# 20 blocks of u of each layer split by ScalarE and GpSimd during the scores, candidate sums by segments, a third PSUM bank for u

## The chip, the cores and the metric

One core of one Trainium2 chip runs the whole program. The metric is device time in microseconds, from one launch to its end. The engines are TensorE (PE; its weight loads PEld), VectorE (DVE), ScalarE (ACT), GpSimd (POOL) and SyncE (SP), which only issues DMA.

## The reference

One inference step of two layers for 512 prompt tokens and 8 sample tokens of width 1024. A layer is a mixer, a layer norm, PEER, and a layer norm. Layer 0 mixes with gated DeltaNet and RG-LRU, layer 1 with sliding-window attention. PEER looks experts up by product keys:

```python
q = (tb @ w_q).reshape(PEER_BLOCK, PEER_HEADS, 2, PEER_D_SUB)
s = jnp.einsum('thcd,hcnd->thcn', q, sub_keys).astype(F32)
s_top, i_top = lax.top_k(s, PEER_TOPK)
cand = (s_top[:, :, 0, :, None] + s_top[:, :, 1, None, :]).reshape(PEER_BLOCK, PEER_HEADS, -1)
cand_idx = (i_top[:, :, 0, :, None] * PEER_N_KEYS + i_top[:, :, 1, None, :]).reshape(
    PEER_BLOCK, PEER_HEADS, -1)
best, pos = lax.top_k(cand, PEER_TOPK)
expert = jnp.take_along_axis(cand_idx, pos, axis=-1)
gate = jax.nn.softmax(best, axis=-1)
act = jax.nn.gelu(jnp.einsum('td,thkd->thk', tb, u_tab[expert]).astype(F32))
return jnp.einsum('thk,thkd->td', (gate * act).astype(tb.dtype), v_tab[expert])
```

There are 8 heads of 2 halves, 128 keys a half, top 16 of each, and 16384 experts (rows of `u_tab` and `v_tab`).

## The kernel before

**Precision.** A float32 matrix is used as a float16 high half and a float16 low half: `split` copies the source, scaled, to the high half on ScalarE (`wh`), and VectorE subtracts to get the low half (`wl`). `mm3` then makes three float16 matmuls (L86 to L88) in place of one.

**PEER for most tokens is dense.** For the first 384 tokens all 128 blocks of u (128 experts each) are multiplied with the tokens: `u_step` takes one block, 24 matmuls of 384 columns into one PSUM bank of the pool `pu` (2 buffers), and ScalarE's gelu writes `act`. The gates of these tokens are spread to a dense table in DRAM (`GD`), in 12 parts of 32 tokens (`gates`): VectorE builds one-hot rows `oh` (L486 to L489), TensorE multiplies them into `pg` (64 matmuls of 128 columns a part), ScalarE copies `pg` eight times to the single buffer `stage`, and a DMA on ScalarE's queue stores `stage` to `GD`. Later the main loop multiplies gate times activation with blocks of v into `yps` (L607), and does the blocks of u that are left, one an iteration. The last 128 prompt tokens and the 8 samples fetch their rows instead: 136 lists of 128 rows for u and as many for v, each by one indirect DMA that GpSimd issues (L357), with a dot product (L364) or a multiply-add on VectorE for each list.

**The order of a layer.** The mixer; the scores (16 steps `hc`: a projection by a block of `wq`, loaded two steps ahead and split, then the product with the keys, `psc`, copied to `scs`, then the top 16 on VectorE, `topk_half`); then `topk_pairs` six times (once for the samples, twice with 4 heads, three times with 8): it makes the 50 candidate sums (`cand`, L256) and index sums (`ce`, L260), one add for each first index and segment, and the lookup of the 16 best. Between them `run_u` does 3, 3, 3 and 7 blocks of u; 7 more stand ahead of each later `pairs`. In `gates` three blocks of u are spread over a part (`UG` is 3). The tile framework orders each engine's instructions when it builds, by its own estimate, so blocks of u move up and down against this text; an engine then runs its list strictly in order.

**The presplit.** `NPRE` is (16, 12): that many blocks of u of a layer are split during the mixer, in quarters, to `ppr`, and stored to DRAM (`PW`) as halves (L106 load of `pst`, L110 store). `ublock` loads these as halves (`wpr`); a later block is loaded as float32 (`wst`) and split when it is needed. All these loads and stores are issued by SyncE, one after the other.

## Time and profile before

| | us |
|---|---|
| median of 3 runs | 3012.0 (3011.1 to 3014.87) |
| the profiled execution | 3010.7 |
| its span, first to last instruction | 3008.9 |
| TensorE busy | 2845.8 (95%) |
| VectorE busy | 2569.4 (85%) |
| ScalarE busy | 1319.3 (44%) |
| GpSimd busy | 856.1 (28%) |
| mean granted clock of TensorE | 0.98 |

Ends of matmuls are modelled, so TensorE's busy time is not time at its peak. The clock is the share of 2.4 GHz that was granted; it has two levels, 1.2 and 2.4 GHz, so a mean of 0.93 is 14% of a stretch at the lower one. In a row of the table by stretch stand the stretch and its length, then busy time and count of instructions for each engine. In a row of one line or tile stand the shortest, median and longest duration in ns and the first and last start in us. In a row of waits stand the waiting instruction, what ended the wait, the total in us, how often, and the longest. A chain that ended last is followed back from the last instruction, at each step to what released it.

### The profile page before, as it was taken

The numbers are of one execution on the slowest core, as the hardware profiler recorded it, in microseconds if no ns is written. First come the engines' busy times: TensorE is split into PE (matmuls) and PEld (weight loads), VectorE is DVE, ScalarE is ACT, GpSimd is POOL, SyncE is SP. The second block draws the span as 40 slices with busy tenths as digits, with TensorE's granted clock in tenths as the row PEclk, the third lists the DMA queues.
The fourth block names the chain that finished last, engine by engine and source line by source line (L and its number), as shares of the span: only waits on it lengthen the run. The fifth ranks groups of instructions, "written<-read, shape, count | busy, mean of one in ns | idle before, by whom it ended". The sixth has DMA issues, their size and how long they took to land.

```text
span 3008.9 us, 49598 instructions
## 1 busy us (share of the span) xinstructions
PE 2845.8 (95%) x18198; PEld 1726.9 (57%) x18198; DVE 2569.4 (85%) x5871; ACT 1319.3 (44%) x2171; POOL 856.1 (28%) x662
## 2 busy tenths in 40 slices
PE   8979999899999999999998899989999999999998
PEld 7768586456655555544446559645665555554443
DVE  6756789999978988889995879989987898898998
ACT  4743332356753333333335743335765333333342
POOL 2300101310024555435520000130002555454552
PEclk9999999999999999999999999999999999999999
DMA  4264424866699999999977422686569999999996
GB/s 136 72 218 149 147 86 161 295 238 217 217 339 390 366 354 363 363 358 370 352 276 246 154 79 85 211 293 213 193 216 327 390 360 360 353 359 359 362 357 234
DMA packets 332104, 798.78 MB, mean 265 GB/s; under 512 B 28611, under 2 KB 165259, under 8 KB 328020
## 3 DMA queue, kind: packets, MB, share of 16 engines
q1 hardware_dynamic: 241004, 442.78, 43.5%
q0 software_dynamic: 78336, 285.25, 25.5%
q10 hardware_dynamic: 12520, 67.58, 6.1%
q8 instruction: 142, 2.33, 0.3%
q14 instruction: 102, 0.84, 0.1%
HBM read 700.96 MB, written 93.17 MB: 264 GB/s over the span
## 4 chain that ended last, share of the span: by engine, by line
PE 66%; DVE 13%; DMA 10%; ACT 6%; issue 4%; POOL 1%; SPq 0%; ACTq 0%; DVEq 0%; POOLq 0%
PE yps L607 30%; PE pu L88 7%; PE pu L86 7%; PE pu L87 7%; DMA row<-in_u_rows,elist 2%; ACT stage L72 2%; PE pq L87 2%; DMA GD<-stage 2%; PE pq L86 2%; PE pq L88 2%; DVE wl L81 2%; DMA pst<-in_uT 2%; DVE row L364 1%; DMA PW<-ppr 1%; DMA gl<-GD 1%
## 5 line engine op out<-in xcount | busy, mean ns | idle before, releaser
L607 PE MATMUL yps<-vv,vw 128*128 128x512 f16 x4536 | 1010.8, 379 | 10.3 <-ACT vv L72 8.1
L607 PEld LDWEIGHTS <-vw 128*128 128x128 f16 x4608 | 450.4, 98 | 542.2 <-issue 17.0
L357 POOL DMA_INDIRECT row<-in_v_rows,elist x272 | 395.4, 1454 | 862.9 <-issue 251.0
L88 PE MATMUL pu<-xh,wl 128*128 128x384 f16 x1824 | 598.4, 329 | 34.2 <-DVE wl L81 33.7
L86 PE MATMUL pu<-xh,wh 128*128 128x384 f16 x1824 | 598.9, 328 | 15.6 <-ACT act L333 10.7
L87 PE MATMUL pu<-xl,wh 128*128 128x384 f16 x1824 | 598.4, 328 | 0.0
L357 POOL DMA_INDIRECT row<-in_u_rows,elist x272 | 389.1, 1430 | 679.8 <-DVE best L237 250.3
L72 ACT ACTIVATE wh<-wst 128x1024 f16<-128x1024 f32 x296 | 312.4, 1056 | 565.3 <-PE pu L87 340.3
L81 DVE SCALAR_TENSOR_TENSOR wl<-wst,wh 128x1024 f16<-128x1024 f32 x296 | 361.7, 1223 | 154.1 <-ACT wh L72 148.1
L88 PEld LDWEIGHTS <-wl 128*128 128x128 f16 x2912 | 287.4, 99 | 186.9 <-DVE wl L81 47.5
L86 PEld LDWEIGHTS <-wh 128*128 128x128 f16 x2912 | 290.1, 100 | 159.3 <-ACT wh L72 25.5
L87 PEld LDWEIGHTS <-wh 128*128 128x128 f16 x2912 | 287.6, 99 | 149.3 <-issue 14.5
L72 ACT ACTIVATE vv<-row 128x1024 f16<-128x1024 f32 x252 | 263.1, 1048 | 232.9 <-PE yps L607 182.6
L81 DVE SCALAR_TENSOR_TENSOR vv<-row,vv 128x1024 f16<-128x1024 f32 x252 | 307.6, 1221 | 49.9 <-ACT vv L72 48.1
L545 DVE SCALAR_TENSOR_TENSOR yac<-row,wgt,yac 128x1024 f32<-128x1024 f32 x268 | 343.5, 1282 | 4.5 <-DMA row<-in_v_rows,elist 2.6
L364 DVE CUSTOM_DVE_ANT_0 row<-row,xtok 128x1024 f32<-128x1024 f32 x256 | 308.4, 1220 | 20.3 <-DMA row<-in_u_rows,elist 20.1
L72 ACT ACTIVATE vw<-act 128x384 f16<-128x384 f32 x256 | 129.7, 516 | 350.8 <-PE yps L607 298.1
L72 ACT ACTIVATE stage<-pg 128x512 f32<-128x512 f32 x192 | 183.4, 1105 | 76.2 <-DMA GD<-stage 65.6
L79 DVE TENSOR_TENSOR vw<-act,vw 128x384 f16<-128x384 f32 x256 | 139.8, 553 | 24.3 <-ACT vw L72 23.6
L333 ACT ACTIVATE act<-pu 128x384 f32<-128x384 f32 x256 | 122.3, 478 | 48.4 <-PE pu L88 46.2
L87 PE MATMUL pq<-xl,wh 128*128 128x264 f16 (+1 forms) x480 | 132.9, 277 | 0.5 <-DVE xl L79 0.3
L88 PE MATMUL pq<-xh,wl 128*128 128x264 f16 (+1 forms) x480 | 132.9, 277 | 0.0
(501 smaller groups left out, 3968.4 us busy)
## 6 DMA issues: line engine op xcount, KB each, us to landing
row<-in_v_rows SPq DMA_DIRECT2D x256, 512.0 KB, 7.8
wst<-in_uT SPq DMA_DIRECT2D x228, 512.0 KB, 6.3
GD<-stage ACTq DMA_DIRECT2D x24, 2048.0 KB, 7.6
gl<-GD SPq DMA_DIRECT2D x64, 768.0 KB, 7.9
wst<-in_wq SPq DMA_DIRECT2D x32, 512.0 KB, 3.4
pst<-in_uT SPq DMA_DIRECT2D x56, 256.0 KB, 4.1
PW<-ppr SPq DMA_DIRECT2D x56, 256.0 KB, 2.9
wpr<-PW SPq DMA_DIRECT2D x28, 512.0 KB, 5.2
```

The costliest lines, as they stand in the source:

```text
L72: self.nc.scalar.activation(out, in_, AF.Copy, scale=scale)
L79: eng.tensor_sub(lo, src, hi)
L81: eng.scalar_tensor_tensor(lo, src, scale, hi, op0=OP.mult, op1=OP.subtract)
L86: mm(out, wh, xh, start=start, stop=False)
L87: mm(out, wh, xl, start=False, stop=False)
L88: mm(out, wl, xh, start=False, stop=stop)
L333: S.activation(t, ps[:, 0:ND], AF.Gelu_apprx_tanh, scale=1.0 / SCW)
L357: G.indirect_dma_start(out=r, out_offset=None, in_=src, in_offset=bass.IndirectOffsetOnAxis(ap=elist[:, k:k + 1], axis=0))
L364: V.tensor_tensor_reduce(u, u, self.xtok[:, 0] if k < P else xrep, 1.0, 0.0, OP.mult, OP.add, hd[:, k:k + 1])
L545: V.scalar_tensor_tensor(dst, vbuf.pop(n), wgt[:, k:k + 1], dst, op0=OP.mult, op1=OP.add)
L607: T.matmul(yps[t][:, o], w[:, a, c], v[:, b, o], start=x == 0 and k == 0, stop=x == P - 1 and k == 2)
```

## The change

- No block of u is split in the mixers (`NPRE` is (0, 0)). Instead 20 blocks a layer (`NPOOL`) are split during the 16 steps of the scores: SyncE loads a block to `gst` (3 buffers, two blocks ahead), ScalarE scales it in place and copies it to the high half in `gpr` (2 buffers), GpSimd subtracts for the low half, SyncE stores both to `PW`.
- `topk_pairs` adds candidates by segments that share a range, 7 adds for `cand` (16 before) and 20 for `ce` (33 before).
- In the stage of the gates the pool for `pt` and `pg` gives one bank of `pt` back, and every third block of u uses it.
- In `gates` two of a part's three blocks of u stand ahead of its copies to `stage`, which are put behind the activation of the second (`behind`), and one stands in the middle; before, one each after the third, sixth and eighth group of four tokens.

The diff:

```diff
@@ -45,3 +45,6 @@
             if b1 > b0:
-                seg.append((a, b0, b1))
+                if seg and seg[-1][1:] == (a, b0, b1):
+                    seg[-1] = (seg[-1][0], a + 1, b0, b1)
+                else:
+                    seg.append((a, a + 1, b0, b1))
                 perm += [start[a] + b for b in range(b0, b1)]
@@ -52,2 +55,4 @@
 LSEG, LCNT, LPERM = lookup_order()
+
+CSEG = [(a0, a1, 0, TOPK // a1) for a0, a1 in ((0, 1), (1, 2), (2, 3), (3, 4), (4, 5), (5, 8), (8, 16))]
 SCW = 1024.0
@@ -98,2 +103,15 @@
 
+    def presplit_load(self, pool, layer, b):
+        st = pool.tile([P, KB, P], F32, name="gst", bufs=3)
+        self.nc.sync.dma_start(st, self.A["uT"][layer, b])
+        return st
+
+    def presplit_pool(self, pool, layer, b, st):
+
+        o = pool.tile([P, 2, KB, P], F16, name="gpr", bufs=2)
+        self.copy(st, st, SCW)
+        self.copy(o[:, 0], st)
+        self.nc.gpsimd.tensor_sub(o[:, 1], st, o[:, 0])
+        self.nc.sync.dma_start(self.PW[layer, b], o)
+
     def presplit(self, pool, layer, n):
@@ -111,4 +129,16 @@
 
+    def behind(self, ins):
+
+        ctx = ExitStack()
+        for i in ins:
+            ctx.enter_context(self.tc.issue_after(i))
+        return ctx
+
+    def last_on(self, *engines):
+
+        ins = self.nc.cur_bb.bb.instructions
+        return [next(i for i in reversed(ins) if i.engine == e.engine) for e in engines]
+
     def ublock(self, layer, b):
-        if b < self.NPRE[layer]:
+        if b < self.NPRE[layer] + self.NPOOL:
             t = self.wst.tile([P, 2, KB, P], F16, name="wpr", tag="wst")
@@ -252,12 +282,14 @@
         ce = pool.tile([P, HM, NC50], F32, name="ce%d" % HM)[:, 0:H]
-        off = 0
-        for a in range(TOPK):
-            nb = TOPK // (a + 1)
-            V.tensor_add(cand[:n, :, off:off + nb], st[:, 0, :, a:a + 1].to_broadcast([n, H, nb]), st[:, 1, :, 0:nb])
-            off += nb
-        off = 0
-        for a, b0, b1 in LSEG:
-            V.tensor_add(ce[:n, :, off:off + b1 - b0], fx[:n, 0, :, a:a + 1].to_broadcast([n, H, b1 - b0]),
-                         fx[:n, 1, :, b0:b1])
-            off += b1 - b0
+
+        def sums(out, x, segs):
+
+            off = 0
+            for a0, a1, b0, b1 in segs:
+                s = [n, H, a1 - a0, b1 - b0]
+                o = out[:n, :, off:off + s[2] * s[3]].rearrange("p h (a b) -> p h a b", a=s[2])
+                V.tensor_add(o, x[:n, 0, :, a0:a1, None].to_broadcast(s), x[:n, 1, :, None, b0:b1].to_broadcast(s))
+                off += s[2] * s[3]
+
+        sums(cand, st, CSEG)
+        sums(ce, fx, LSEG)
         best = pool.tile([P, HM, TOPK], F32, name="best%d" % HM)[:, 0:H]
@@ -314,2 +346,3 @@
         nprep, nu, live = [0], [0], [0]
+        third = []
 
@@ -326,3 +359,3 @@
             h, l = upair.pop(u)
-            ps = pu.tile([P, 512], F32, name="pu")
+            ps = (third[0] if third and u % 3 == 2 else pu).tile([P, 512], F32, name="pu")
             for kb in range(KB):
@@ -392,2 +425,4 @@
             wb = self.epair[1]
+            npool = [0]
+            gst = [self.presplit_load(tp, layer, self.NPRE[layer] + k) for k in range(2)]
             for hc in range(16):
@@ -419,2 +454,8 @@
                     self.topk_half(st[:, t, c, h], ix[:, t, c, h], wk, sc[:, t])
+                while npool[0] < self.NPOOL * (hc + 1) // 16:
+                    b = self.NPRE[layer] + npool[0]
+                    npool[0] += 1
+                    if npool[0] + 1 < self.NPOOL:
+                        gst.append(self.presplit_load(tp, layer, b + 2))
+                    self.presplit_pool(tp, layer, b, gst.pop(0))
 
@@ -435,4 +476,5 @@
                 tc.tile_pool(name="pairs", bufs=1, side="right", reuse_waits="tile") as tp, \
-                tc.tile_pool(name="topkps", bufs=2, space=bass.MemoryType.PSUM, reuse_waits="tile") as psum:
+                tc.tile_pool(name="topkps", bufs=1, space=bass.MemoryType.PSUM, reuse_waits="tile") as psum:
             lts = {}
+            third.append(psum)
 
@@ -475,2 +517,4 @@
                 stage = gp.tile([P, P, TG], F32, name="stage")
+                run_u(us - 1)
+                order = self.last_on(S)
                 for t4 in range(0, TG, 4):
@@ -494,4 +538,6 @@
                         T.matmul(pg[:, k], oh[:, 0, q, :, r], oh[:, 3, q, :, r], start=False, stop=True)
-                    self.copy(stage[:, :, t4:t4 + 4].rearrange("p i t -> p t i"), pg)
-                    if t4 * us // TG < (t4 + 4) * us // TG:
+                    with self.behind(order):
+                        self.copy(stage[:, :, t4:t4 + 4].rearrange("p i t -> p t i"), pg)
+                    order = []
+                    if t4 == TG // 2:
                         run_u(1)
@@ -529,2 +575,3 @@
             run_u(P)
+        third.clear()
         kctx.close()
@@ -1530,4 +1577,4 @@
             self.GD = dp.tile([12, P, P, 32], F32, name="GD")
-            self.NPRE = (16, 12)
-            self.PW = dp.tile([2, max(self.NPRE), P, 2, KB, P], F16, name="PW")
+            self.NPRE, self.NPOOL = (0, 0), 20
+            self.PW = dp.tile([2, max(self.NPRE) + self.NPOOL, P, 2, KB, P], F16, name="PW")
             self.AD = dp.tile([self.NSP, P, ND], F32, name="AD")
```

How the scheduler places this is seen on ScalarE. In the first place, one step `hc` in the middle of layer 0's scores, there stood before a copy of a `wq` block to its high half, the two evacuations of the projection `pq`, that of the scores `psc` and that of the samples' scores `ss`:

```order
L72 ACTIVATE wh<-wst 128x1024
L72 ACTIVATE q<-pq 128x256
L72 ACTIVATE q<-pq 128x264
L72 ACTIVATE scs<-psc 128x512
L72 ACTIVATE ss<-psc 128x8
```

and there stand now:

```order
L77 ACTIVATE gpr<-gst 128x1024
L77 ACTIVATE gst<-gst 128x1024
L77 ACTIVATE gpr<-gst 128x1024
L77 ACTIVATE wh<-wst 128x1024
L77 ACTIVATE q<-pq 128x256
L77 ACTIVATE q<-pq 128x264
L77 ACTIVATE gst<-gst 128x1024
L77 ACTIVATE scs<-psc 128x512
L77 ACTIVATE ss<-psc 128x8
```

Four copies of 1024 columns of u (`gst` in place, `gpr` the high half) came in, ahead of the copies that TensorE waits for and between them; over all 16 steps they are 40.

The second place is behind the scores of layer 0, from the exponential of the second half of the last token tile (`gexp` with 64 columns a partition) on. Before, with the activations `act` of blocks of u and the first split `wh` of a block of u:

```order
L270 ACTIVATE gexp_6313<-gexp_6313 128x64
L333 ACT_TABLE_LOAD
L333 ACTIVATE act<-pu 128x384 x2
L368 ACTIVATE wgt<-hd 128x8
L333 ACTIVATE act<-pu 128x384 x4
L72 ACTIVATE wh<-wst 128x1024
```

Now:

```order
L302 ACTIVATE gexp_6131<-gexp_6131 128x64
L366 ACT_TABLE_LOAD
L366 ACTIVATE act<-pu 128x384 x3
L401 ACTIVATE wgt<-hd 128x8
L366 ACTIVATE act<-pu 128x384 x4
L302 ACT_TABLE_LOAD
L302 ACTIVATE gexp_6444<-gexp_6444 128x128
L366 ACT_TABLE_LOAD
L366 ACTIVATE act<-pu 128x384 x2
L401 ACTIVATE wgt<-hd 128x8
L366 ACTIVATE act<-pu 128x384
L77 ACTIVATE wh<-wst 128x1024
```

Before, the first split of a block of u stood behind 15 activations and ahead of the exponential of the next `pairs` (128 columns a partition); now it stands behind 19, and that exponential comes first.

The third place is a late part of the gates of layer 1, from one store of `stage` to the next. Before:

```order
L498 DMA GD<-stage 128x4096
L72 ACTIVATE wh<-wst 128x1024
L333 ACTIVATE act<-pu 128x384
L72 ACTIVATE stage<-pg 128x4x128 x4
L72 ACTIVATE wh<-wst 128x1024
L333 ACTIVATE act<-pu 128x384
L72 ACTIVATE wh<-wst 128x1024
L333 ACTIVATE act<-pu 128x384
L72 ACTIVATE stage<-pg 128x4x128 x4
L498 DMA GD<-stage 128x4096
```

Now:

```order
L544 DMA GD<-stage 128x4096
L77 ACTIVATE wh<-wst 128x1024
L366 ACTIVATE act<-pu 128x384
L77 ACTIVATE wh<-wst 128x1024
L366 ACTIVATE act<-pu 128x384
L77 ACTIVATE stage<-pg 128x4x128 x4
L77 ACTIVATE wh<-wst 128x1024
L366 ACTIVATE act<-pu 128x384
L77 ACTIVATE stage<-pg 128x4x128 x4
L544 DMA GD<-stage 128x4096
```

One split and activation moved from between the two groups of copies to `stage` to ahead of them.

On the other engines the lists before the first one-hot `oh` of a layer, counted from the first `MAX` of the scores, change like this: VectorE's splits `wl` are 20 in either layer (before 29 in layer 0 and 35 in layer 1), its dot products 29 (35 and 36), its candidate adds 35 + 100 (80 + 165). GpSimd has 20 subtractions `gpr<-gst,gpr` in a row, ahead of the first gather. In the gates, 72 activations `act` stand ahead of the twelfth store (75 and 76), and 4, 4, 5, 5, 4 and then six times 3 between the stores.

## Rows read from the trace of the kernel before

**Rows 1.** By stretch: us; busy PE, PEld, DVE, ACT, POOL; clock, DMA share, GB/s.

```profile
160.00:250.00 90.00, 75.24 (x590) 67.51 (x589) 52.46 (x123) 44.37 (x118) 0.66 (x1) 0.93 0.75 236
250.00:385.00 135.00, 126.44 (x868) 89.45 (x869) 91.36 (x179) 46.75 (x104) 10.05 (x10) 0.95 0.38 126
385.00:480.00 95.00, 95.00 (x857) 85.08 (x855) 85.92 (x516) 30.54 (x70) 0.00 (x0) 0.99 0.27 87
...
520.00:638.00 118.00, 99.94 (x581) 57.27 (x582) 108.28 (x395) 35.81 (x54) 43.37 (x33) 0.96 0.89 303
...
1580.00:1690.00 110.00, 91.78 (x735) 74.49 (x736) 71.79 (x239) 69.60 (x191) 3.89 (x3) 0.91 0.70 224
...
1690.00:1800.00 110.00, 97.11 (x653) 55.34 (x652) 85.16 (x260) 58.37 (x165) 4.56 (x5) 0.96 0.31 103
...
1935.00:2060.00 125.00, 105.14 (x604) 59.90 (x603) 114.09 (x405) 41.47 (x60) 43.23 (x32) 0.95 0.86 291
...
1000.00:1125.00 125.00, 125.00 (x666) 64.96 (x664) 111.09 (x145) 45.45 (x66) 66.45 (x48) 1.00 0.99 363
```

**Rows 2.** Waits of ScalarE, 160 to 250 us: total, times, longest.

```profile
ACT ppr L72 <- DMA PW<-ppr: 23.5, 18, 2.9
```

**Rows 3.** VectorE's first score and first one-hot, layer 0: ns, first to last start.

```profile
L237 DVE MAX8 st<-scs x64: 273/277/295, 393.4 to 487.1; 128x8 f32<-128x128 f32 x64
...
L486 DVE TENSOR_TENSOR oh<-iota,lt x48: 672/686/714, 633.9 to 849.0; 128x1024 f16<-128x1024 f16 x48
```

**Rows 4.** The same in layer 1.

```profile
L237 DVE MAX8 st<-scs x64: 275/280/298, 1807.5 to 1901.2; 128x8 f32<-128x128 f32 x64
...
L486 DVE TENSOR_TENSOR oh<-iota,lt x48: 673/686/726, 2057.3 to 2277.4; 128x1024 f16<-128x1024 f16 x48
```

**Rows 5.** Waits of TensorE, 520 to 640 us.

```profile
PE pu L88 <- DVE wl L81: 12.9, 8, 5.3
```

**Rows 6.** Stores of stage, first and last start, layer 0 and layer 1.

```profile
L498 ACTq DMA_DIRECT2D GD<-stage x12: 326/326/340, 658.0 to 859.8; - x12
...
L498 ACTq DMA_DIRECT2D GD<-stage x12: 326/326/333, 2082.4 to 2290.8; - x12
```

**Rows 7.** Blocks of u finished by the last store, layer 0 and layer 1.

```profile
L333 ACT ACTIVATE act<-pu x75: 466/474/539, 487.8 to 855.7; 128x384 f32<-128x384 f32 x75
...
L333 ACT ACTIVATE act<-pu x76: 459/474/532, 1902.0 to 2286.6; 128x384 f32<-128x384 f32 x76
```

**Rows 8.** The chain that ended last, 2195 to 2295 us.

```profile
2195.01 0.16 PE pu L86
...
2231.65 0.95 ACT wh L72
...
2232.59 0.38 ACT act L333
...
2232.97 3.66 ACT stage L72 x4
...
2236.65 7.72 DMA GD<-stage
```

**Rows 9.** VectorE in order of time, 614 to 622 us: start, us, what.

```profile
615.45 1.22 DVE L81 SCALAR_TENSOR_TENSOR wl<-wst,wh 128x1024 f16<-128x1024 f32 x1
616.59 1.81 DVE L282 TENSOR_REDUCE ev<-eq 128x32 f32<-128x1600 f32 x1
...
620.61 1.21 DVE L260 TENSOR_TENSOR ce<-fx 128x32 f32<-128x32 f32 x13
```

**Rows 10.** The page: one copy on ScalarE, and stores of split halves.

```profile
L72 ACT ACTIVATE wh<-wst 128x1024 f16<-128x1024 f32 x296 | 312.4, 1056 | 565.3 <-PE pu L87 340.3
...
PW<-ppr SPq DMA_DIRECT2D x56, 256.0 KB, 2.9
```

**Rows 11.** GpSimd by shape: count, busy us, mean ns of one.

```profile
L1462 POOL MEMSET qz<- 128x2320 f32 x1 | 2.0, 2022 | 0.0
...
L750 POOL TENSOR_SCALAR_AFFINE_SELECT mt<-ones 128x128 f32<-128x128 f32 x3 | 1.3, 463 | 0.0
```

## The prediction

> **What bounds the kernel now.** I read the page's busy shares first and distrust them: TensorE is called 95% busy, but that is a mean over stages with different limits. So I cut the span into stretches and read each. In the main loop TensorE works without a break (125.00 of 125 us from 1000 us on) [rows 1], the change touches nothing there, and a block of u that is not done before a main loop is done in it, at its full price. What can be won is TensorE's idle time elsewhere, and three places have some.
>
> First the mixers. From 160 to 250 us TensorE is busy 75.24 of 90 us, from 1580 to 1690 us 91.78 of 110, and its mean granted clock is 0.93 and 0.91, so it spends part of them at its lower level, 1.2 GHz [rows 1]. These are the stretches in which the presplit runs. In the first, ScalarE waits 18 times, 23.5 us together, until a store of presplit halves has landed and it may write the next; whatever the mixer has queued behind that copy waits too [rows 2].
>
> Second the stretch from the first score to the first one-hot. VectorE starts the top-k of the scores at 393.4 us and the first one-hot of the gates at 633.9 us [rows 3], in layer 1 at 1807.5 and 2057.3 us [rows 4]. In between it is the engine that sets the pace: 85.92 of 95 us during the scores, 108.28 of 118 us after them, 114.09 of 125 in layer 1 [rows 1]. TensorE runs ahead into u and stops where a low half isn't there: 12.9 us in 8 waits for `wl` [rows 5]. So this stretch gets shorter by what VectorE has less to do, and by no more.
>
> Third the gates. Twelve parts run from the first store of `stage` at 658.0 us to the last at 859.8 us, and from 2082.4 to 2290.8 us in layer 1 [rows 6], with 75 and 76 blocks of u finished by then [rows 7]. Where a part has three blocks of u, ScalarE's order binds it: the single `stage` buffer must land in DRAM (7.72 us), then come four copies (3.66 us), the splits and activations that stand between (0.95 + 0.38 us a block), and four more copies [rows 8].
>
> **The change, part by part.**
>
> Presplit out of the mixers. If idle TensorE time from 160 to 250 us (16%) fell to the 6% of the stretch behind it (8.56 of 135 us), 75.24 us of work would take 80 us: 10 us gained, and 2 more for the clock (0.93 to 0.95) [rows 1]. In mixer C the neighbour (1690 to 1800 us) idles 12%: 91.78 / 0.88 = 104 us, 6 us gained, and 2 for the clock. Together 20 us. The lower bound is 0: that work is a row of small dependent matmuls and may keep its gaps. The upper bound is all idle time (14.8 + 18.2 us) and the time lost at the lower level (half of 2 x 0.07 x 90 and of 2 x 0.09 x 110, 6 + 10 us): 49 us. Behind it on SyncE stand the loads of `S`, which can only come earlier.
>
> VectorE before the first one-hot. From the order: layer 0 has 9 splits `wl` fewer there (29 to 20), layer 1 has 15 fewer (35 to 20), and 6 and 7 dot products move behind it. One split holds VectorE 1.14 us (615.45 to 616.59) [rows 9], a dot product is as long. The candidate sums fall from 16 + 33 adds a call to 7 + 20; five of the six calls of a layer stand ahead of the one-hot, so 110 adds go. In a row 13 take 1.21 us [rows 9], 0.09 each; the merged adds keep the elements, so I take 0.07 us, 8 us a layer. Layer 0: 9 x 1.14 + 6 x 1.14 + 8 = 25 us. Layer 1: 15 x 1.14 + 7 x 1.14 + 8 = 33 us.
>
> What the new split costs there. ScalarE gets 40 copies of 1.06 us a layer [rows 10], 42 us into 95 us of scores in which it is busy 30.5 us [rows 1]: room enough. GpSimd's subtraction isn't in the trace. A fill of 2320 elements takes 2.02 us, 0.87 ns each, so not under 0.9 us; a select that reads and writes 128 elements takes 0.46 us, which makes 3.7 us for 1024 [rows 11]. It is nearer to the select: I take 3.0 us. The two `gpr` buffers give one block per half of (copy 1.06 + subtraction 3.0 + store). A store of half the size lands in 2.9 us [rows 10], so 2.9 to 5.8 us, a period of 3.5 to 4.9 us against the 95 / 20 = 4.75 us wanted: 0 to 4 us a layer. I take 4, since 21 MB more pass in those 95 us (221 GB/s on top of 87 [rows 1]). SyncE sends the `wq` loads behind stores that wait for GpSimd, but they run two ahead. GpSimd's gathers stand behind all 20 subtractions, and need the scores anyway.
>
> Does the subtraction slow VectorE beside it? No row shows two such operations at once. If it stops none, that costs nothing; if it holds the splits `wl`, each of 14 in the scores meets a running one with 20 x 3.0 / 95 = 63% and waits 1.5 us: 13 us a layer. I take the middle of 0 and 13, 7 us. The Trainium skill, SBUF — State Buffer, section "SBUF: two separate sides", speaks against the change here: VectorE with two SBUF inputs and a GpSimd instruction that reads SBUF exclude each other for a whole instruction. By that rule it would be the whole 13 us, and the top-k operations, of one input, would be left alone. The Trainium skill, GPSIMD Engine Reference, section 3.1, measures 4.497 us for a two-input operation on 2048 fp32 elements, an estimate of 2.25 us here; by it the sum would be a few us lower, and no run here shows it yet.
>
> So the one-hot comes 25 - 11 = 14 us earlier in layer 0 and 33 - 11 = 22 us in layer 1.
>
> The gates. A block of u costs 24 x 0.16 = 3.9 us of TensorE [rows 8], the 64 matmuls of a part, a third of the columns each, 3.4 us. By the new order the parts up to the sixth store have 4, 4, 5, 5, 4 blocks: 3 x 19.0 + 2 x 22.9 = 103 us. The last six have 3, now with two blocks ahead of the copies, under the landing, and one between: 7.72 + 2 x 3.66 + 1.33 = 16.4 us, 98 us, and 201 us in all for 40 blocks. Layer 0 had most of its parts so already and took 201.8 us for 39, so I take one block more, 205 us; layer 1 had two blocks between and took 208.4 us for 38. The third bank I take at nothing: VectorE and this chain bind, not the bank.
>
> **Sum.** Layer 0: the last store is at 658.0 - 14 + 205 = 849 us instead of 859.8, but 72 blocks are done by then instead of 75, and 3 x 3.9 = 11.7 us go into the main loop: 1 us lost. Layer 1: 2082.4 - 22 + 205 = 2265.4 instead of 2290.8, 4 blocks later, 15.6 us: 10 us gained. With the mixers 20 + 10 - 1 = 29 us. The profiled execution took 3010.7 us (span 3008.9 and 1.8 around it), so 2981.7; the median is 1.3 us above it: **2983 us**. About 0.2%, 6 us, can be told from no change.
>
> **The rivals.**
> - *GpSimd holds VectorE altogether.* If every subtraction stopped whatever VectorE does, a layer would lose 20 x 3.0 = 60 us in place of 7: 2 x 53 us more, 3089 us, slower. It decides from 7 + 29 / 2 = 21.5 us a layer, 1.1 us a subtraction. For it: VectorE binds just there. Against it: the top-k operations read one tensor. Chance 0.09.
> - *GpSimd holds the splits `wl`, and only these.* 13 us a layer in place of 7, 2983 + 12 = 2995 us. For it: a split reads two tensors, as the subtraction does. Against it: ScalarE and GpSimd may settle into a rhythm with the splits. Chance 0.14. This is what the rule of the Trainium skill's SBUF — State Buffer amounts to here.
> - *Nothing is lost beside the scores.* Then 22 us more are gained, 2961 us; with the mixers at their upper bound 2932. For it: ScalarE and the DMA queues are half idle there [rows 1]. Chance 0.22.
> - *The mixers give nothing.* Their small matmuls wait for each other, and the stores merely filled the gaps: 3003 us. For it: 12% idle where no presplit runs. Chance 0.14.
> - *No change.* The mixers give nothing and the work saved on VectorE before the one-hot comes back as waits for the gathers: 3012 us. Chance 0.08.
>
> The forecast itself (2968 to 2990 us) has 0.33. Faster by over 0.2%: 0.33 + 0.14 + 0.22 and most of the mixers' case, 0.80; within: 0.11; slower: 0.09. The range 2943 to 3008 us leaves out the first rival, the lowest part of the third and most of the last, some 0.2.
>
> **What the next profile should show.** TensorE's idle time from 160 to 250 us under 8 us, and no wait of ScalarE for `PW`. The first one-hot, counted from the first score, after 226 us in layer 0 (240.5 before) and 228 in layer 1 (249.8 before); splits `wl` in the scores with some longer than 1.22 us. GpSimd's subtraction near 3 us. Twelve stores within 205 us, 72 blocks of u by the last. I am wrong if the scores last longer than 110 us, if `MAX8` rows lengthen beside GpSimd, or if the stretch before the one-hot shrinks by what TensorE, not VectorE, no longer waits for.

## The result, and the profile after

The changed kernel takes 2961.2 us (median of 6 runs, 2952.8 to 2970.3), the kernel before 3012.1 beside it: ratio 0.983, 95% interval 0.9815 to 0.985, 51 us faster. The forecast was 2983 us. The profiled execution took 2954.8 us (span 2953.1, mean granted clock 0.989), 6 us under the median.

TensorE by stretch, the columns as in [rows 1]: the first mixer, the scores, what follows them up to the first one-hot, and the second mixer.

```profile
160.00:250.00 90.00, 88.76 (x756) 83.86 (x755) 39.47 (x79) 32.07 (x70) 1.08 (x2) 0.96 0.23 77
...
370.30:465.00 94.70, 92.36 (x825) 81.54 (x824) 87.84 (x497) 63.36 (x106) 38.41 (x18) 1.00 0.74 264
480.00:587.00 107.00, 92.49 (x544) 53.12 (x542) 97.56 (x382) 29.97 (x47) 39.65 (x32) 0.95 0.89 311
1555.00:1665.00 110.00, 98.80 (x841) 80.45 (x842) 69.54 (x245) 67.40 (x180) 3.94 (x3) 0.97 0.44 144
```

TensorE is idle 1.2 us from 160 to 250 us, where it was 14.8, and no wait of ScalarE for `PW` stands there any more [rows 1, 2]. The whole of each mixer shows more than these stretches do. The kernel before, from the start to layer 0's first projection `pq`, and from the last `yps` of layer 0 to layer 1's first projection:

```profile
0.00:383.30 383.30, 338.96 (x2711) 275.14 (x2712) 260.71 (x579) 186.54 (x384) 53.04 (x100) 0.96 0.45 142
1575.20:1798.50 223.30, 189.15 (x1391) 129.87 (x1389) 160.62 (x506) 128.28 (x356) 9.37 (x9) 0.94 0.50 164
```

The changed kernel between the same events:

```profile
0.00:358.70 358.70, 329.79 (x2711) 268.89 (x2712) 239.22 (x515) 165.42 (x320) 52.35 (x100) 0.98 0.34 111
1550.40:1750.80 200.40, 180.08 (x1390) 126.66 (x1389) 142.59 (x457) 113.05 (x307) 9.46 (x9) 0.98 0.37 121
```

Counted by matmuls and not by time, the forecast's two pieces of the first mixer, the stretch with the presplit and the neighbour behind it, were before:

```profile
160.30:251.20 90.90, 74.94 (x589) 67.49 (x588) 53.66 (x125) 45.41 (x120) 0.66 (x1) 0.93 0.76 237
251.20:383.30 132.10, 125.08 (x863) 88.68 (x864) 88.86 (x176) 44.71 (x99) 10.05 (x10) 0.95 0.37 123
```

and are now, with the same counts of matmuls (to one at an edge):

```profile
160.10:231.00 70.90, 70.18 (x590) 65.79 (x589) 33.51 (x63) 25.43 (x58) 0.54 (x1) 0.95 0.21 71
231.00:358.70 127.70, 120.25 (x864) 84.18 (x864) 87.37 (x173) 44.08 (x97) 9.56 (x10) 0.99 0.43 145
```

The mixers' matmuls are as many as before (2711, and 1391 against 1390). The mixers are 24.6 and 22.9 us shorter; 15.4 and 13.8 us of it are TensorE's idle time (length less busy time), the rest as many matmuls at a higher mean clock.

Then the events that answer to [rows 3, 4, 6, 7], layer 0 and layer 1 (first and last start in us):

```profile
L267 DVE MAX8 st<-scs x64: 270/278/297, 370.3 to 464.8; 128x8 f32<-128x128 f32 x64
L530 DVE TENSOR_TENSOR oh<-iota,lt x48: 672/686/706, 587.3 to 813.7; 128x1024 f16<-128x1024 f16 x48
L544 ACTq DMA_DIRECT2D GD<-stage x12: 326/326/340, 615.2 to 824.2; - x12
L366 ACT ACTIVATE act<-pu x72: 469/474/523, 465.5 to 820.0; 128x384 f32<-128x384 f32 x72
...
L267 DVE MAX8 st<-scs x64: 268/277/295, 1762.5 to 1857.6; 128x8 f32<-128x128 f32 x64
L530 DVE TENSOR_TENSOR oh<-iota,lt x48: 671/686/716, 1978.5 to 2206.0; 128x1024 f16<-128x1024 f16 x48
L544 ACTq DMA_DIRECT2D GD<-stage x12: 326/327/333, 2007.0 to 2216.4; - x12
```

From the first score to the first one-hot 217.0 us (240.5 before) and 216.0 (249.8); the twelve stores within 209.0 us (201.8) and 209.4 (208.4), 72 blocks of u by the last. From the first projection of layer 0 to the last `yps` of its main loop it is 1191.7 us (1191.9 before), from that of layer 1 to the end of the span 1202.3 (1210.4). So all that the change does behind the mixers is worth 8 us, and the mixers make the other 47.5 of the 56 us between the two profiles; the medians differ by 51.

GpSimd's subtraction, which no row of before showed (ns: shortest, median, longest):

```profile
L114 POOL TENSOR_TENSOR gpr<-gst,gpr x40: 2123/2136/3068, 361.8 to 1832.3; 128x1024 f16<-128x1024 f32 x40
```

### The profile page after: what moved, and what is told of

It reads as the page before. It is cut to its first block, busy times and chain, and to the rows that moved or that the text cites. A ratio compares the mean times of both kernels' runs of the same rounds, so it can differ in the third digit from the quotient of the medians.

```text
span 2953.1 us, 49153 instructions
## 1 busy us (share of the span) xinstructions
PE 2824.2 (96%) x18198; PEld 1714.9 (58%) x18198; DVE 2501.0 (85%) x5483; ACT 1351.7 (46%) x2127; POOL 956.7 (32%) x702
## 3 DMA queue, kind: packets, MB, share of 16 engines
q1 hardware_dynamic: 229228, 455.37, 44.7%
## 4 chain that ended last, share of the span: by engine, by line
PE 59%; DMA 13%; DVE 12%; ACT 7%; issue 6%; POOL 3%; ACTq 0%; SPq 0%; POOLq 0%; DVEq 0%
PE yps L654 24%; PE pu L93 7%; PE pu L91 7%; PE pu L92 7%; DMA row<-in_u_rows,elist 3%; DMA gl<-GD 3%; ACT stage L77 2%; POOL row L390 2%; DMA gst<-in_uT 1%; DVE row L397 1%; ACT wh L77 1%; DVE wl L86 1%; PE psg L1034 1%; DMA row<-in_v_rows 1%; PE pg L538 1%
## 5 line engine op out<-in xcount | busy, mean ns | idle before, releaser
L93 PE MATMUL pu<-xh,wl 128*128 128x384 f16 x1728 | 565.8, 329 | 28.5 <-DVE wl L86 28.1
L91 PE MATMUL pu<-xh,wh 128*128 128x384 f16 x1728 | 567.5, 328 | 21.7 <-ACT wh L77 21.7
L92 PE MATMUL pu<-xl,wh 128*128 128x384 f16 x1728 | 566.9, 328 | 0.0
L86 DVE SCALAR_TENSOR_TENSOR wl<-wst,wh 128x1024 f16<-128x1024 f32 x284 | 351.3, 1240 | 165.8 <-ACT wh L77 151.7
L77 ACT ACTIVATE wh<-wst 128x1024 f16<-128x1024 f32 x284 | 299.3, 1054 | 403.5 <-PE pu L92 293.3
L91 PEld LDWEIGHTS <-wh 128*128 128x128 f16 x2816 | 279.9, 99 | 166.3 <-ACT wh L77 39.1
L93 PEld LDWEIGHTS <-wl 128*128 128x128 f16 x2816 | 277.5, 99 | 168.5 <-DVE wl L86 38.5
L92 PEld LDWEIGHTS <-wh 128*128 128x128 f16 x2816 | 277.7, 99 | 132.8 <-issue 5.9
L84 DVE TENSOR_TENSOR vw<-act,vw 128x384 f16<-128x384 f32 x256 | 139.3, 553 | 13.8 <-ACT vw L77 13.4
L640 DVE TENSOR_TENSOR act<-act,gl 128x384 f32<-128x384 f32 x256 | 127.6, 552 | 11.2 <-DMA gl<-GD 9.1
```

Source lines behind the costliest of these rows:

```text
L77: self.nc.scalar.activation(out, in_, AF.Copy, scale=scale)
L84: eng.tensor_sub(lo, src, hi)
L86: eng.scalar_tensor_tensor(lo, src, scale, hi, op0=OP.mult, op1=OP.subtract)
L91: mm(out, wh, xh, start=start, stop=False)
L92: mm(out, wh, xl, start=False, stop=False)
L93: mm(out, wl, xh, start=False, stop=stop)
```

## The experiments

All kernels compute the whole reference; the two `mix_dead` split some blocks a second time for nothing. The account in the last columns is an estimate worked out from each profile: idle is the span less TensorE's busy time; the loss by the clock is the span times (1 - mean granted clock), since the lower of the two levels is half the higher; the rest is what is left. The mean clock has three decimals here, so each loss is good to 1.5 us.

| kernel | median, us | ratio to before, 95% interval | span | idle | clock | rest |
|---|---|---|---|---|---|---|
| before | 3012.1 | | 3008.9 | 163.1 | 51.2 | 2794.6 |
| changed | 2961.2 | 0.983 (0.9815 to 0.985) | 2953.1 | 128.9 | 32.5 | 2791.7 |
| mixers_only | 3009.5 | 1.000 (0.998 to 1.001) | 3008.5 | 171.5 | 45.1 | 2791.9 |
| mix_dead | 3018.2 | 1.002 (1.001 to 1.004) | 3016.6 | 162.3 | 57.3 | 2797.0 |
| mix_dead_nostore | 2994.8 | 0.994 (0.992 to 0.996) | 2991.5 | 147.9 | 47.9 | 2795.7 |
| no_presplit | 2984.0 | 0.991 (0.989 to 0.994) | 2983.4 | 143.6 | 47.7 | 2792.1 |
| sums_only | 3015.3 | 1.002 (1.000 to 1.004) | 3013.6 | 160.9 | 57.3 | 2795.4 |
| sums_old | 2990.8 | 0.994 (0.992 to 0.996) | 2994.0 | 152.6 | 44.9 | 2796.5 |
| sums_old_f | 2980.6 | 0.990 (0.987 to 0.992) | 2980.4 | 142.7 | 44.7 | 2793.0 |
| gates_old | 2971.0 | 0.987 (0.985 to 0.989) | 2970.8 | 133.9 | 41.6 | 2795.3 |
| gates_new | 3008.8 | 1.000 (0.999 to 1.002) | 3016.5 | 165.3 | 57.3 | 2793.9 |
| pool24 | 2963.3 | 0.984 (0.982 to 0.987) | 2967.1 | 134.5 | 41.5 | 2791.1 |
| pool24_g | 2953.8 | 0.981 (0.979 to 0.984) | 2948.8 | 124.2 | 35.4 | 2789.2 |
| pool28 | 2978.3 | 0.990 (0.987 to 0.992) | 2978.8 | 141.2 | 41.7 | 2795.9 |

The rest is 2789 to 2797 us in all fourteen. A block of u costs TensorE the same wherever it stands; what an edit is worth is what it takes from TensorE's idle time and from its time at 1.2 GHz, no more. This is what the readings below go by.

### Is it the mixers? mixers_only

```diff
-            self.NPRE = (16, 12)
+            self.NPRE = (0, 0)
```

> The kernel before, with NPRE (0, 0) and nothing else: no block of u is split ahead, all are split by VectorE when they are needed. Theory: the presplit cost the mixers all that the changed kernel shows there (first projection of layer 0 at 358.7 us instead of 383.3, mixer C 22.9 us shorter: 47.5 us), half of it idle TensorE and half its lower clock. Then the same 47 us go here, and 16 + 12 splits of 1.14 us (32 us) come back on VectorE ahead of the one-hot: 3012 - 47 + 32 = 2997 us, first projection at 359 us, granted clock of mixer C 0.98. Rival, my forecast: the mixers are worth 20 us, the rest of their gain came with something else of the change: 3012 - 20 + 32 = 3024 us, first projection near 371 us.

Measured 3009.5 us, no change. The mixers did what the theory says: first projection at 359.1 us, mixer C 203.3 us (223.3 before), 44 us together. But 28 splits went back to VectorE, and their price is not the 32 us of the splits alone: from the first store of `stage` to the first `yps` TensorE idles 26.7 and 27.1 us in the two layers, 8.8 and 14.2 before. So the mixers' 44 us are real, and were paid back in full behind them, 12 us more than the theory had. The order of the gates, below, may have a part in the price: the last four parts of layer 0 take 17.9 to 19.5 us, where they took 15.9 to 16.2.

### What in the presplit slows a mixer? mix_dead, mix_dead_nostore

The changed kernel, with 16 and 12 blocks split in the mixers as well, into a buffer that nothing reads; in the second the store is left out.

```diff
-                self.presplit(pre, 0, self.NPRE[0])
+                self.presplit(pre, 0, 16)
...
-                self.presplit(pre, 1, self.NPRE[1])
+                self.presplit(pre, 1, 12)
...
-                nc.sync.dma_start(self.PW[layer, b, :, :, c], o)
+                nc.sync.dma_start(self.PX[layer, b, :, :, c], o)
```

> The changed kernel with the presplit of before put back into the mixers (16 and 12 blocks: loads, copies, subtractions, stores), but into a DRAM buffer that nothing reads, so that all behind the mixers stays as changed. Theory: the presplit alone made the mixers longer, by 47 us: 2961 + 47 = 3008 us, the first projection of layer 0 again near 383 us, mixer C near 223 us, TensorE idle 44 us and at its lower clock 30 us ahead of that first projection (29 and 14 in the changed kernel). Rival, my forecast: 20 us, 2981.

> The same without the stores: the halves are made and never stored, so that ScalarE never waits for a buffer to land in DRAM. Theory: those waits (18 of them, 23.5 us in layer 0) hold up the copies that the mixer has queued behind them on ScalarE; without them most of the 47 us is gone, 2961 + 10 = 2971 us. Rival: the copies and subtractions themselves stand between dependent steps of the mixer in the queues of ScalarE and VectorE; the stores change little, 3000 us or more.

The mixers of mix_dead by the stage table:

```profile
0.00:385.40 385.40, 343.33 (x2710) 278.71 (x2711) 260.83 (x579) 186.60 (x383) 53.50 (x100) 0.95 0.46 145
1585.90:1809.10 223.20, 186.59 (x1390) 130.03 (x1389) 160.16 (x506) 127.97 (x355) 10.16 (x9) 0.96 0.51 167
```

and of mix_dead_nostore:

```profile
0.00:373.50 373.50, 338.65 (x2711) 275.96 (x2712) 261.22 (x579) 185.77 (x383) 52.10 (x100) 0.96 0.40 127
1567.30:1778.70 211.40, 182.67 (x1391) 126.53 (x1390) 160.38 (x506) 127.26 (x355) 10.03 (x9) 0.98 0.44 145
```

With the work back, both mixers are as long as before (385.4 and 223.2 us). Without the stores about half of it goes (373.5, 211.4). ScalarE's waits from 140 to 385 us say part of what the stores did; with them:

```profile
ACT ppr L77 <- DMA PX<-ppr: 26.9, 19, 3.1
```

and 9.0 us more for the loads of `pst`; without:

```profile
ACT ppr L77 <- DMA pst<-in_uT: 18.9, 14, 9.1
```

In mixer C the profile shows no wait of ScalarE for a store to land, only waits for the loads, with the stores and without them:

```profile
ACT ppr L77 <- DMA pst<-in_uT: 23.6, 13, 3.2
```

```profile
ACT ppr L77 <- DMA pst<-in_uT: 14.9, 9, 4.0
```

and yet this mixer is 11.8 us shorter without the stores. So neither side had it alone: half goes with the stores, but the wait for a buffer to land is not the whole way in which they cost, since mixer C loses as much without that wait. At least three things go together with a store here, and no run took them apart. The first is that wait. The second is its place on SyncE, which also issues the mixer's loads: VectorE waits 14.7 us for `S` in the first mixer with the stores, 6.0 without. The third is the order of the instructions: TensorE's matmuls of the first mixer stand in mix_dead as they stood before, all 2710 of them, but in mix_dead_nostore they go another way from the 1372nd on, and in the changed kernel from the 1359th on. The other half stays while copies (20 us more of ScalarE in the first mixer), subtractions (22 us more of VectorE) and loads stay, which no run took apart either. mix_dead as a whole lost 57 us, ten more than expected; its gates are 7 and 6 us longer, with the longer form of their late parts that is described below.

### The split beside the scores: no_presplit, pool24, pool28

```diff
-            self.NPRE, self.NPOOL = (0, 0), 20
+            self.NPRE, self.NPOOL = (0, 0), 0
```

(24 and 28 in the other two; without blocks the first two loads of `gst` are left out.)

> The changed kernel with no block of u split ahead at all (NPOOL 0), the rest as changed. Theory: 20 splits of 1.14 us come back on VectorE ahead of the one-hot of each layer, 46 us, less what the scores get back (4 us between first projection and first score, 5 us of splits held by GpSimd): 2961 + 37 = 2998 us; the splits in the scores are all 1.22 us long. Rival: the split beside the scores takes as much as it saves, since ScalarE, GpSimd and the DMA queues delay what TensorE waits for: 2961 us within 6.

> The changed kernel with 28 blocks of u split during the scores in place of 20. Theory: ScalarE gets 17 us more (88 of 100 us), GpSimd 17 more (60), both still free in time; 8 splits of 1.14 us a layer leave VectorE ahead of and in the gates, and TensorE stops less for low halves (14.6 and 13.7 us idle from the last score to the one-hot): 2949 us. Rival: ScalarE comes late with copies that TensorE waits for in the scores, and more splits are held by GpSimd: the scores lengthen by over 5 us a layer and eat the gain, 2961 us or more.

> The changed kernel with 24 blocks of u split during the scores. In the list of ScalarE the last five parts now have one activation ahead of the copies to stage and two behind. Theory: 2 us for each of these parts (20 us), 4 us a layer for longer scores (28 blocks cost 10.3 and 6.5 us), against 4 splits a layer less on VectorE (8 us): 2961 + 20 = 2981 us. Rival: only the scores and splits count, 2961 us within 6.

Without it 2984.0 us: the split beside the scores is worth 23 us, less than the theory's 37. With 28 blocks 2978.3 us, 17 us worse, as its rival says. The scores of pool28:

```profile
373.50:478.30 104.80, 98.10 (x854) 84.29 (x852) 88.61 (x496) 80.45 (x125) 56.43 (x26) 1.00 0.91 323
```

They last 10.3 us longer than in the changed kernel, and TensorE, busy without a gap in the scores of the kernel before [rows 1] and idle 2.3 us in them in the changed kernel, idles 6.7 us. But this is not where the 17 us went. From the first score to the first one-hot TensorE idles 14.8 and 12.1 us in the two layers, less than in the changed kernel (17.0 and 15.2), and the one-hot comes 7 and 9 us earlier. What grew is behind it. From the first store to the first `yps` of layer 0, pool28 and then the changed kernel:

```profile
610.30:862.10 251.80, 234.46 (x1850) 152.11 (x1849) 217.87 (x357) 155.58 (x198) 22.70 (x17) 0.99 0.71 255
```

```profile
615.20:852.30 237.10, 225.80 (x1825) 149.58 (x1824) 208.86 (x378) 156.64 (x197) 10.59 (x8) 0.99 0.68 244
```

TensorE idles 17.3 us there in place of 11.3 (15.4 and 11.6 in layer 1), 6 us more in layer 1's main loop, and 9 us more of the profile are the clock. The rival's condition held, its way to the loss did not, and why more blocks split ahead lengthen the gates no run tested. With 24 blocks the time is that of 20 (2963.3 us), where the theory said 20 us more: the order of the gates got worse, as it says, and something made up for it; that it was the blocks fits pool24_g below, but is not shown.

### The sums, and the order in which the gates come out: sums_only, sums_old, sums_old_f

sums_only is the kernel before with the segments, sums_old the changed kernel without:

```diff
-        sums(cand, st, CSEG)
-        sums(ce, fx, LSEG)
+        off = 0
+        for a in range(TOPK):
+            nb = TOPK // (a + 1)
+            V.tensor_add(cand[:n, :, off:off + nb], st[:, 0, :, a:a + 1].to_broadcast([n, H, nb]), st[:, 1, :, 0:nb])
...
```

> The kernel before with the candidate and index sums by segments and nothing else. Theory: VectorE sets the pace between the scores and the one-hot, and the merged adds save the 17.8 us a layer that the changed kernel's rows show (ce 27.4 to 16.6, cand 13.4 to 6.4): 3012 - 35 = 2977 us, the one-hot 17 us after the first score earlier in either layer. Rival, my forecast: 8 us a layer, 2996 us. Rival: the saved time comes back as waits for the gathers of rows or for TensorE, 3012 us.

> The changed kernel with the candidate and index sums of before (16 and 33 adds a call). Theory one, VectorE's pace: 17.8 us a layer more on VectorE ahead of the one-hot come out whole, 2961 + 35 = 2996 us. Theory two, which the sums alone on the kernel before speak for (no gain there): TensorE finishes other blocks of u meanwhile, and only what TensorE stands idle counts: 2961 to 2968 us, the one-hot later but with 4 blocks more done. Between them, from no_presplit against mixers_only (26 us for sums, gates and bank together) less the 10 us of gates and bank: 2977 us.

The 17.8 us a layer in these expectations are a misreading of mine: durations of adds that overlap were added up. VectorE's busy time tells it right, 2569.4 us before and 2547.5 in sums_only: 11 us a layer for six calls, about 9 for the five ahead of the one-hot.

On the kernel before the sums gained nothing, 3015.3 us (ratio 1.000 to 1.004); in the changed kernel they are worth 30 us. One thing that differs is an order that nobody wrote. In the last five parts of the gates the scheduler either lets two blocks of u stand ahead of the copies to `stage`, or one, and it decides that by what comes long before. ScalarE in one such part of the changed kernel, from store to store:

```profile
2184.74 0.33 ACTq L544 DMA_DIRECT2D GD<-stage  x1
2185.18 1.06 ACT L77 ACTIVATE wh<-wst 128x1024 f16<-128x1024 f32 x1 [0.48 <-DVE oh L532]
2186.15 0.47 ACT L366 ACTIVATE act<-pu 128x384 f32<-128x384 f32 x1
2186.52 1.05 ACT L77 ACTIVATE wh<-wst 128x1024 f16<-128x1024 f32 x1
2187.47 0.48 ACT L366 ACTIVATE act<-pu 128x384 f32<-128x384 f32 x1
2191.95 3.76 ACT L77 ACTIVATE stage<-pg 128x512 f32<-128x512 f32 x4 [4.00 <-PE pu L92]
2195.49 1.07 ACT L77 ACTIVATE wh<-wst 128x1024 f16<-128x1024 f32 x1
2196.45 0.48 ACT L366 ACTIVATE act<-pu 128x384 f32<-128x384 f32 x1
2196.82 3.77 ACT L77 ACTIVATE stage<-pg 128x512 f32<-128x512 f32 x4
2200.62 0.33 ACTq L544 DMA_DIRECT2D GD<-stage  x1
```

and of sums_old, whose text of the gates is the same:

```profile
2225.83 0.33 ACTq L540 DMA_DIRECT2D GD<-stage  x1
2226.28 1.06 ACT L74 ACTIVATE wh<-wst 128x1024 f16<-128x1024 f32 x1 [0.48 <-DVE oh L528]
2227.24 0.47 ACT L362 ACTIVATE act<-pu 128x384 f32<-128x384 f32 x1
2233.79 3.71 ACT L74 ACTIVATE stage<-pg 128x512 f32<-128x512 f32 x4 [6.08 <-DMA GD<-stage]
2237.30 1.05 ACT L74 ACTIVATE wh<-wst 128x1024 f16<-128x1024 f32 x1
2238.25 0.48 ACT L362 ACTIVATE act<-pu 128x384 f32<-128x384 f32 x1
2238.61 1.06 ACT L74 ACTIVATE wh<-wst 128x1024 f16<-128x1024 f32 x1
2239.56 0.50 ACT L362 ACTIVATE act<-pu 128x384 f32<-128x384 f32 x1
2239.93 3.80 ACT L74 ACTIVATE stage<-pg 128x512 f32<-128x512 f32 x4
2243.75 0.33 ACTq L540 DMA_DIRECT2D GD<-stage  x1
```

In both the copies wait for the store before to land. The 4.00 us that the first list puts down to TensorE are such a wait too: the last product `pg` ahead of these copies had ended at 2188.51 us, and the copies start 7.1 to 7.2 us after the store in all ten such parts of the changed kernel, in four of which the profile names the landing. With two blocks ahead, two splits and activations run under the landing (7.21 us here) and one stands between the copies: 15.9 us. With one ahead, ScalarE has nothing for 6.08 us of a landing of 7.96 us, and two stand between: 17.9 us. Of these 2.0 us, 1.3 are the block between the copies and 0.75 the longer landing, for which no run shows a cause. The kernel before had the short form in layer 0 and the long one in layer 1; sums_only had them the other way round and lost 13.6 us in layer 0 from the first projection to the end of the main loop and won 8.3 in layer 1; that the order did this is not tested in these two.

sums_old_f ties the copies of the last four parts to an activation that makes the order short, and changes nothing in layer 0 ahead of it (`acts` collects the activations; nine more blocks stand in the text ahead of the gates, so that the tie binds):

```diff
-                order = self.last_on(S)
+                n = {8: 65, 9: 68, 10: 71, 11: 74}.get(4 * t + part)
+                order = [acts[n - 1].ins] if n else []
```

> The changed kernel with the sums of before, and with the first copy to stage of the parts 9 to 12 tied behind a given activation, so that two activations stand ahead of the four copies there and one behind them, as in the changed kernel, where sums_old had one ahead and two behind. Everything that the two have in layer 0 before part 9 stands in the same order. Theory: the sums themselves are worth little, and sums_old lost its 30 us mostly to that order: parts with two activations ahead take 15.9 us, those with one 17.9, 4 parts a layer: 16 us less than sums_old, 2975 us. Rival: the order of these rows does nothing, the 30 us are VectorE's work for the sums: 2991 us.

2980.6 us: 10 us come back of the 16 expected, the last four parts of layer 0 at 16.0 to 16.2 us and three of layer 1 at 15.9 to 16.1. So the order is a third of what the sums seemed to be worth. The other 19 us are not settled: from the first score to the one-hot TensorE's idle time differs by 2 us between sums_old_f and the changed kernel, in the gates by 8 us, and by the mean clock their profiles differ by 12 us. The sums on VectorE cannot be told there from the orders that they bring about.

### The gates and the bank: gates_old, gates_new, pool24_g

gates_old takes the order and the bank out of the changed kernel, gates_new puts both into the kernel before:

```diff
-                run_u(us - 1)
-                order = self.last_on(S)
...
-                    if t4 == TG // 2:
+                    if t4 * us // TG < (t4 + 4) * us // TG:
```

> The changed kernel with the gates as before: blocks of u one each after the third, sixth and eighth group of tokens, and two buffers for pt and pg, no third bank for u. Theory: TensorE is the bound of the gates in either order (busy 247.85 of 259.70 us from the first pg to the first yps in layer 0), so that order and bank are worth nothing: 2961 us within 6. Rival, my forecast: they are worth about 9 us in layer 1 and nothing in layer 0, 2970 us. Rival: they cost what layer 0 shows from its first one-hot to its last store (236.9 us against 225.9), less two blocks of u of 3.9 us: 2958 us or, with both layers, 2954.

> The kernel before with the third bank and the new order of the gates alone. In the list of ScalarE the last five parts have two activations ahead of the copies in layer 0, as before, and one in layer 1, as before too, since the scheduler lets blocks of u run ahead of the text and the tie does not bind. Theory: no gain, 3011 us within 6; late parts 16 us in layer 0 and 18 in layer 1. Rival, my forecast for this part of the change: layer 1 gains 9 us, 3002 us.

> pool24 with the first copy to stage of the parts 9 to 12 tied behind a given activation, two ahead of the copies as in the changed kernel; the lists stand as in pool24 up to part 8. Theory: 4 parts of 2 us a layer, 16 us less than pool24, about 2965 us. Rival: nothing, as pool24.

gates_old took 2971.0 us: the new gates are worth 10 us in the changed kernel, where I had 9, though in both layers and not in layer 1 alone. Its last five parts take 17.5 to 18.6 us. gates_new gained nothing (3008.8 us): its late parts came out at 16.0 to 16.2 us in layer 0 (the last at 17.6) and at 17.8 to 18.1 in layer 1, nearly as in the kernel before, and in layer 1 one split and activation still stand ahead of the copies: blocks of u run ahead of the text, so the tie to "the second block of this part" does not bind. pool24_g, tied by number as sums_old_f is, took 2953.8 us against pool24's 2963.3, with 16 us in place of 18 in its last four parts. Its ratio (0.979 to 0.984) overlaps that of the changed kernel (0.9815 to 0.985): the fastest of the kernels here, but not told apart from it.

## Why the prediction was right, and where it was not

The sign and the range held; the narrower band of the forecast itself, 2968 to 2990 us, did not. The forecast was 22 us too high, and nearly all of this is one term.

**The mixers, mis-sized.** "Together 20 us" was worked out from two stretches whose idle share would fall to that of the stretch behind. The nine kernels without presplit in the mixers have their first projection at 358.7 to 364.7 us and a mixer C of 199 to 205 us, the four with all of it at 380.0 to 387.1 and 222 to 226. The means differ by 21 and 22 us, 43 together. In the profile of the changed kernel 29 us of 47 are idle time, where I took 16, and 18 the clock, where I took 4. The rule "idle as in the neighbour" failed. The presplit ran from 177 to 253 us and from 1597 to 1688 us, so the neighbours had none, and what they idle stayed without it: by the rows above 7.0 us before and 7.4 us now in the first mixer (12.8 and 10.9 in mixer C). The stretch with the presplit did not fall to that neighbour's 6% but to 1% (16.0 us idle before, 0.7 now), and took 70.9 us where 80 were forecast; that of mixer C fell from 16.8 us idle of 108.7 to 4.6 of 91.7, to 5% where 12% were forecast. The clock was mis-sized too: for mixer C the prediction's own rows, 0.91 to 0.96 over 110 us, give 5 us and not 2, and the neighbours, for which the sum had nothing, gained 4.4 and 6.1 us, most of it in busy time at a higher clock (0.95 to 0.99 and 0.96 to 1.00). The two stretches themselves gave 20 and 17 us. The upper bound of 49 us, which counted them alone, was nearer than the forecast; the lower one, that small matmuls keep their gaps, is refuted.

**VectorE before the one-hot: the work saved was right, its side costs were not.** VectorE's busy time from the first score to the one-hot fell by 22.6 us in layer 0 and 31.7 in layer 1; I had 25 and 33 less 7 for held splits. Of the 11 us of side costs the pacing cost 1 (first to last `MAX8` 94.5 us, 93.7 before), and the held splits 2.5 a layer, in place of 7.

**GpSimd's subtraction** takes 2.14 us; I took 3.0. The Trainium skill, GPSIMD Engine Reference, section 3.1, gave an estimate of 2.25 us, which the trace bears out to 5%.

**Does it stop VectorE?** Yes, the splits, and whole. GpSimd and VectorE in the changed kernel (start, us):

```profile
380.75 2.13 POOL L114 TENSOR_TENSOR gpr<-gst,gpr 128x1024 f16<-128x1024 f32 x1 [0.86 <-ACT gpr L77]
```

```profile
381.02 0.29 DVE L271 FIND_INDEX8 ix<-st,swork 128x8 uint32<-128x128 f32 x1
381.23 0.08 DVE L271 MATCH_VALUE_LOAD ix<-st,swork 128x8 f32 x1
381.28 0.29 DVE L271 FIND_INDEX8 ix<-st,swork 128x8 uint32<-128x128 f32 x1
381.66 2.31 DVE L86 SCALAR_TENSOR_TENSOR wl<-wst,wh 128x1024 f16<-128x1024 f32 x1
384.23 0.49 DVE L267 MAX8 st<-scs 128x8 f32<-128x128 f32 x2 [0.27 <-ACT scs L77]
```

The split starts at 381.66 and lasts until 383.97: the subtraction's end at 382.88 and 1.08 us more. All eight splits longer than 1.3 us end 1.08 us after a subtraction's end, to 0.01; in the scores of no_presplit the longest is 1.226 us. The top-k operations do not wait: `FIND_INDEX8` beside the same subtraction keeps its 0.29 us, and the 74 `MAX8`, of one input, that start with over 0.3 us of a subtraction to go last 0.27 to 0.30 us. This is the rule of the Trainium skill, SBUF — State Buffer, section "SBUF: two separate sides", and the trace agrees with it. But it costs 2.5 us a layer and not 13, because only 4 of 14 splits a layer meet a subtraction with more than 0.2 us to go (in pool28 it is 3.2 and 7.6 us). That ScalarE makes both high halves one after the other, so that the two rarely start together, is how I read it; no run tested it.

**The gates.** The last six parts took 97.7 us (98 forecast), the first five 111.3 (103), and from the first one-hot to the first store it is 27.9 us in place of 24.1. These 12 us ate what the one-hot had won beyond the forecast, 9.5 and 11.8 us. With them the two layers behind the mixers come to 8 us, where I had 9 (1 lost, 10 gained): that sum was right, but by two errors of one size. The third bank at nothing was not tested alone.

**Why the earlier one-hot is worth so little.** It comes 23.5 and 33.8 us earlier (14 and 22 forecast), but TensorE's idle time ahead of it fell by 1.1 and 4.6 us only (240.5 less 222.48, then 217.0 less 200.04; 249.8 less 229.94, then 216.0 less 200.77). 27 blocks of u were done by then where it had been 32 in layer 0; they were done later, at the same price. I named VectorE the engine that sets the pace there, and beside a TensorE busy 92% of the time that is half of it.

**The rivals.** "Nothing is lost beside the scores" has the measured time, 2961 us, and its condition nearly held (3.5 us lost a layer), but the 22 us did not come from there. "The mixers give nothing" and "no change" fall with the 43 us; "GpSimd holds VectorE altogether" falls with the `MAX8` rows. "GpSimd holds the splits, and only these" is what happens, at 2.5 us a layer and not at its price of 13.

## What to carry to other kernels

Where movable work fills one engine, price every edit by what it takes from that engine's idle time and low clock, not by how much earlier some other engine gets somewhere: here fourteen kernels agree within 8 us on all the rest. Background work put "into gaps" of a stage of small dependent steps shares its in-order queues and lengthens it: it cost 43 us here, about half of it with the stores alone. Beside the scores it was worth 23 us with 20 blocks; 24 did no more, and 28 lost 17 us of it. Where a scheduler orders the instructions, look at the order of a repeated part after every edit, even one far away: one block ahead of or behind a copy was 2 us a part.

## What the runs showed of the hardware that was not expected

Identical mixers do not run at the same clock. gates_old has the first mixer of the changed kernel, TensorE's matmuls in the same order, and took 4.9 us longer to the first projection, at a mean clock of 0.96 in place of 0.98:

```profile
0.00:363.60 363.60, 334.52 (x2711) 273.27 (x2712) 239.25 (x515) 165.84 (x320) 52.34 (x100) 0.96 0.34 110
```

Its idle time is the same (29.1 us, 28.9 in the changed kernel); the busy time differs by 4.7 us. Runs of one kernel here differ by up to 23 us (the kernel before, 2998.8 to 3021.5), so a profile is read beside the median, and a few us in one profile are not an effect.

A subtraction that meets a running split waits as the split does: the longest, 3.07 us, started at 1783.30 us, while a split ran from 1783.18 to 1784.38. It and the three others above 2.2 us each end 1.99 us after the end of the split that they met.
